# The first seven-product tile of each half layer: another order of its products, and one step of its sums of x moved

## The chip, the cores and the metric

The kernel runs on one core of a Trainium2 chip. The metric is the device time of one execution in microseconds; the time of a kernel is the median of its runs. Five engines take part: PE (TensorE, matmuls; PEld are its weight loads), DVE (VectorE), ACT (ScalarE), POOL (GpSimd) and SP (SyncE, which issues most of the DMAs). Each has its own list of instructions, and semaphores make one wait for another.

## The reference

One inference step of a two-layer decoder: 512 prompt tokens and 8 sample tokens, model width 1024, hidden width 2816, all in float32. Each layer is half a SwiGLU, a token mixer (causal pooling in layer 0, windowed attention in layer 1), and another half SwiGLU:

```python
def _rmsnorm(x, g):
    y = xf * lax.rsqrt(jnp.mean(xf * xf, axis=-1, keepdims=True) + EPS)
    return (y * g.astype(jnp.float32)).astype(x.dtype)

def _swiglu(x, wg, wu, wd):
    return (jax.nn.silu(x @ wg) * (x @ wu)) @ wd
...
        x = x + 0.5 * _swiglu(_rmsnorm(x, norm_g[l, 0]), ffn_w_gate[l, 0], ffn_w_up[l, 0], ffn_w_down[l, 0])
        h = _rmsnorm(x, norm_g[l, 1])
...
        x = x + 0.5 * _swiglu(_rmsnorm(x, norm_g[l, 2]), ffn_w_gate[l, 1], ffn_w_up[l, 1], ffn_w_down[l, 1])
```

So there are four SwiGLU blocks, called half layers 1 to 4 here (`fi` 0 to 3 in the code). They are most of the work and the place of the change.

## The kernel before

**Layout.** Activations are held transposed: the 1024 features in eight tiles of 128 partitions, and 520 tokens along the free dimension, cut into two halves of H = 260. Each value is split into a high part in fp32r (ScalarE, a copy) and a low part (VectorE, value minus high part), and each product is three matmuls: high x high, high x low, low x high (`terms`). Weights are split in the same way, in pieces of 128 x 512: L260 (ACT) makes `wh`, L261 (DVE) makes `wl`.

**Half layers.** The 2816 hidden features are 22 tiles of 128, in parts of 8, 8 and 6. For each part the gate and up tiles come first, one hidden tile j at a time, and then the down projection. The first NPL = (4, 3, 2, 3) hidden tiles of each half layer are plain (`plain_tile`: four pieces of weights, 24 matmuls each). From tile j = NPL on, `strassen_tile` computes gate and up together by a scheme of seven products of 2 x 2 blocks instead of eight. The blocks of the weights are A11, A12 (gate, lower and upper 512 features of x) and A21, A22 (up); the blocks of x are B11, B12 (lower features, token half 0 and 1) and B21, B22 (upper). The seven products, each 12 matmuls of 128x260 at L563, are A11 B11, S1 T1, S2 T2, A12 B21, S4 B22, S3 T3 and A22 T4. S1 to S4 are sums of weight blocks, T1 to T4 sums of x.

**Sums of the weights** (`Weights.combos`, `sums`). S1 and S3 are formed by accumulating DMAs on POOL's queue (L191, L192). S2 is S1 added onto A11 in place (L197, DVE), S4 is S2 added onto A12 in place (L201, DVE); so A11 must be split before S2 is formed, and A12 before S4. `sums` lists the pieces of a tile in the order in which the products take them: A11, S1, (A22 of the tile before), S2, A12, S4, S3; A22 follows in the next tile's list. Weights are split up to five pieces ahead (`prefetch`), in six buffers.

**Sums of x** (`sums` inside `yoco_step`, L780 to L801). A generator of eight steps, two for each k of 0 to 3. The first scales two tiles of x (L787, ACT, twice), makes t1 and t2 (L792, L793, DVE) and splits them into `th` and `tl` (L319, L320) as pair k; the second makes t3 and t4 (L797, L798) and splits them as pair k + 4. T1 and T2 are the halves of pairs 0 to 3, T3 and T4 those of pairs 4 to 7. L792 and L797 are kept in program order (`later`).

**Hooks.** A plain tile calls one hook after each piece of its weights. `start_hooks` gives the list for half layers 1, 2 and 4: `none` once or twice, `norm` (the norm's token sums, `rstd_tok`, and the first step), `none`, `norm_all` (the norm R over all tokens, and `known`, which releases the plain tiles that wait for R), and then seven steps. Half layer 3 starts its steps earlier, beside the K/V projection, and has a list of its own (L1288). `strassen_tile` is called after the remaining hooks are drained.

**Banks.** A double bank (`duo`) has two PSUM banks; four doubles rotate. A seven-product tile takes two: `a` is the first bank of one, `c` both of the other. A11 B11 opens `a`, and after the copy `sa` (L705) S2 T2 adds onto it. S1 T1 opens the second bank of `c`; after the copy `sb` (L707) S4 B22 adds onto it. A12 B21 opens the first bank of `c`. Then gate = silu of (`sa` + `c`) x R: L713, L714, L715. S3 T3 and A22 T4 go on adding in `a` for the up half (L717, L720, L722). The last product of a tile is delayed into the next one (`finish`).

**Order.** In these parts the order of the instructions on each engine is not that of the source: a planner lays it down when the kernel is built, by its own idea of durations, from the dependencies and the place in the source; it may mix the matmuls of two products or of two tiles. Only what is wrapped in `later` keeps its place.

## Time and profile before

| | us |
|---|---|
| median of 3 runs | 1655.13 |
| lowest and highest run | 1652.17, 1657.66 |
| the profiled execution | 1657.26 |
| its span, first to last instruction | 1655.5 |
| mean granted TensorE clock | 0.990 |

The costliest groups are these; a row gives line, engine, operation, names, shapes and count, then busy time, mean ns of one, and the engine's idle time just before them with what ended most of it.

```profile
L260 ACT ACTIVATE wh<-raw 128x512 fp32r<-128x512 f32 (+1 forms) x794 | 465.3, 619 | 262.7 <-PE ps L535 81.3
L261 DVE TENSOR_TENSOR wl<-raw,wh 128x512 fp32r<-128x512 f32 (+1 forms) x794 | 518.0, 675 | 71.1 <-ACT wh L260 69.1
L563 PE MATMUL ps<-th,wh 128*128 128x260 f32 x1216 | 343.7, 284 | 1.5 <-ACT wh L260 1.2
```

Times inside the execution are counted from the first instruction. The first seven-product tiles of the four half layers begin in this execution at 62.88, 438.10, about 802.5 and 1331.57.

### The profile page before, as it was taken

The page shows a single profiled execution, that of the slowest core. Times are in us where ns is not written, and L with a number is a line of the kernel's source. Part 1 is how long each engine was busy: PE and PEld are TensorE (multiplying, and loading weights), DVE is VectorE, ACT ScalarE, POOL GpSimd, SP SyncE. Part 2 cuts the span into 40 slices and gives each one's busy share as a digit, 9 for nine tenths or more (in the row PEclk, how much of TensorE's full clock was granted, in tenths as well). Part 3 has the DMA queues.
Part 4 walks back from the last instruction along what each step waited for, and adds up shares of the span by engine and source line. Part 5 has one row for each costly group of instructions (what it writes and reads, how often), then busy time and mean ns, then how long its engine had stood idle before and what let it go on. Part 6 is the DMA issues. An engine that isn't in the chain of part 4 may idle for free.

```text
span 1655.5 us, 34978 instructions
## 1 busy us (share of the span) xinstructions
PE 1624.3 (98%) x13386; PEld 1607.8 (97%) x13386; DVE 1421.8 (86%) x2817; ACT 980.1 (59%) x2032; POOL 228.9 (14%) x304
## 2 busy tenths in 40 slices
PE   9999999999999999999999999999989999999997
PEld 9999999999999999999999999999989999999997
DVE  6999999887899999888899989886786799999886
ACT  5665665566665565655655665655785565565555
POOL 1111111000111111100211111101110111111100
PEclk9999999999999999999999999999979999999999
DMA  8577878752587887744787877753222567787851
GB/s 225 119 174 180 183 175 176 192 158 87 127 181 176 179 185 176 163 134 103 186 186 178 182 175 173 170 181 91 59 50 75 126 142 176 179 184 173 178 139 52
DMA packets 377363, 254.62 MB, mean 154 GB/s; under 512 B 13134, under 2 KB 343878, under 8 KB 377156
## 3 DMA queue, kind: packets, MB, share of 16 engines
q1 hardware_dynamic: 339390, 187.30, 40.9%
q0 software_dynamic: 34048, 60.00, 22.7%
q10 hardware_dynamic: 3758, 5.09, 1.0%
q8 instruction: 105, 1.72, 0.4%
q14 instruction: 62, 0.51, 0.1%
HBM read 189.76 MB, written 6.11 MB: 118 GB/s over the span
## 4 chain that ended last, share of the span: by engine, by line
PE 90%; DVE 3%; ACT 3%; DMA 1%; issue 1%; POOL 0%; SPq 0%; DVEq 0%; ACTq 0%; POOLq 0%
PE ps L563 64%; PE ps L535 20%; ACT wh L260 1%; DVE wl L261 1%; PE ps L1464 1%; PE ps L1061 1%; DMA pr<-in_bands_dram 1%; PE ps L1086 1%; ACT sm L1408 1%; PE ps L1377 0%; PE ps L1433 0%; PE ps L494 0%; PE ps L1752 0%; PE ps L1759 0%; DMA raw<-in_ffn_w_gate_dram 0%
## 5 line engine op out<-in xcount | busy, mean ns | idle before, releaser
L260 ACT ACTIVATE wh<-raw 128x512 fp32r<-128x512 f32 (+1 forms) x794 | 465.3, 619 | 262.7 <-PE ps L535 81.3
L261 DVE TENSOR_TENSOR wl<-raw,wh 128x512 fp32r<-128x512 f32 (+1 forms) x794 | 518.0, 675 | 71.1 <-ACT wh L260 69.1
L563 PE MATMUL ps<-th,wh 128*128 128x260 f32 x1216 | 343.7, 284 | 1.5 <-ACT wh L260 1.2
L563 PE MATMUL ps<-th,wl 128*128 128x260 f32 x1216 | 342.4, 282 | 0.6 <-DVE wl L261 0.6
L563 PE MATMUL ps<-tl,wh 128*128 128x260 f32 x1216 | 342.3, 282 | 0.0
L563 PE MATMUL ps<-xh,wh 128*128 128x260 f32 x896 | 253.6, 284 | 3.3 <-ACT sb L707 1.8
L563 PE MATMUL ps<-xl,wh 128*128 128x260 f32 x896 | 251.6, 282 | 0.0
L563 PE MATMUL ps<-xh,wl 128*128 128x260 f32 x896 | 250.5, 282 | 0.5 <-DVE wl L261 0.4
L192 POOL DMA_DIRECT2D raw<-raw x108 | 93.1, 862 | 1046.8 <-DVE wl L261 283.5
L563 PEld LDWEIGHTS ps<-th,wh 128*128 128x128 f32 x1216 | 228.4, 188 | 3.7 <-ACT wh L260 2.5
L563 PEld LDWEIGHTS ps<-th,wl 128*128 128x128 f32 x1216 | 228.8, 188 | 0.8 <-DVE wl L261 0.8
L563 PEld LDWEIGHTS ps<-tl,wh 128*128 128x128 f32 x1216 | 229.0, 188 | 0.0
L563 PE MATMUL ps<-hh,wh 128*128 128x260 f32 x656 | 184.7, 285 | 2.4 <-ACT wh L260 1.8
L563 PE MATMUL ps<-hl,wh 128*128 128x260 f32 x656 | 183.8, 283 | 0.2 <-DVE hl L320 0.2
L563 PE MATMUL ps<-hh,wl 128*128 128x260 f32 x656 | 183.1, 282 | 0.0
L563 PEld LDWEIGHTS ps<-xh,wh 128*128 128x128 f32 x896 | 168.3, 188 | 5.3 <-ACT sb L707 2.2
L563 PEld LDWEIGHTS ps<-xh,wl 128*128 128x128 f32 x896 | 168.1, 188 | 0.9 <-DVE wl L261 0.9
L563 PEld LDWEIGHTS ps<-xl,wh 128*128 128x128 f32 x896 | 168.4, 188 | 0.0
L563 PEld LDWEIGHTS ps<-hh,wh 128*128 128x128 f32 x656 | 123.0, 188 | 4.3 <-ACT wh L260 2.8
L563 PEld LDWEIGHTS ps<-hl,wh 128*128 128x128 f32 x656 | 123.3, 188 | 0.4 <-DVE hl L320 0.4
L563 PEld LDWEIGHTS ps<-hh,wl 128*128 128x128 f32 x656 | 123.0, 188 | 0.0
L535 PE MATMUL ps<-hh,wh 128*128 128x260 f32 x572 | 116.3, 285 | 0.6 <-ACT vtok L1245 0.6
(331 smaller groups left out, 3595.2 us busy)
## 6 DMA issues: line engine op xcount, KB each, us to landing
raw<-in_ffn_w_gate_dram SPq DMA_DIRECT2D x87, 512.0 KB, 5.6
raw<-in_ffn_w_up_dram SPq DMA_DIRECT2D x87, 512.0 KB, 5.6
raw<-in_ffn_w_down_dram SPq DMA_DIRECT2D x128, 256.0 KB, 4.4
raw<-raw POOLq DMA_DIRECT2D x108, 256.0 KB, 3.5
S<-raw POOLq DMA_DIRECT2D x108, 256.0 KB, 4.6
S<-in_ffn_w_up_dram SPq DMA_DIRECT2D x76, 256.0 KB, 6.2
raw<-in_ffn_w_down_dram SPq DMA_DIRECT2D x16, 768.0 KB, 4.5
S<-in_ffn_w_down_dram SPq DMA_DIRECT2D x32, 256.0 KB, 4.5
```

Of the source, the lines that this page charges most:

```text
L192: G.dma_start(blk(raw, 2, 1), blk(raw, 1, 1), accum_op=ALU.add)
L260: pin(nc.scalar.activation(dh, src, AF.Copy))
L261: pin(nc.vector.tensor_tensor(dl, src, dh.bitcast(F32), op=ALU.subtract))
L535: ins = T.matmul(banks[:, hf, :H], a[:, kk, :], hcols(b, hf), start=(first and i == 0), stop=(last and i == 2),)
L563: T.matmul(bank[:, :H], a[:, kk, :], b, start=(not more and kk == 0 and i == 0), stop=(kk == 3 and i == 2), skip_group_check=more,)
L1061: T.matmul(o, a[:, s], b[:, kk, :], start=(n == 0), stop=(n == 5))
L1086: T.matmul(po[:, half * 256 : half * 256 + 256], z[:, tau, c], b, start=(i == 0), stop=(i == len(lst) - 1),)
L1408: S.activation(z, z, AF.Exp, scale=-1.0, bias=nm[:, i : i + 1], accum_out=self.den[:, i : i + 1])
L1464: T.matmul(po[:, bi * 256 : (bi + 1) * 256], a, p_[:, kc_], start=(n == 0), stop=(n == 3 * len(kts) - 1),)
```

## The change

It has four parts. (1) For the first seven-product tile of each half layer the weights' pieces are listed as A11, A12, S4, S1, S2, S3; S4's function forms S2 first, once, and S2's piece finds it formed. (2) `strassen_tile` takes the products of that tile in the same order: A11 B11, A12 B21, S4 B22 (all on x itself), then S1 T1, S2 T2, S3 T3, A22 T4. S4 B22 now opens its bank, and S1 T1 goes to the second bank of the double whose first bank is `a`. (3) Since S1 T1 is no longer added in the bank, one new VectorE instruction adds `sb` to the second half of `g`, between L713 and L714. (4) In the hooks of `start_hooks` the `none` between `norm` and `norm_all` becomes a step, and the list ends one step sooner; the number of steps is as before.

```diff
@@ combos
         def s2(raw):
-            V.tensor_tensor(blk(raw, 1, 1), blk(raw, 1, 1), tmp[1], op=ALU.add)
+            if "S2" not in tmp:
+                V.tensor_tensor(blk(raw, 1, 1), blk(raw, 1, 1), tmp[1], op=ALU.add)
+                tmp["S2"] = True
             return blk(raw, 1, 1)
 
         def s4(raw):
+            s2(raw)
             V.tensor_tensor(blk(raw, 1, 2), blk(raw, 1, 2), blk(raw, 1, 1), op=ALU.add)
             return blk(raw, 1, 2)
@@ Weights.sums
-    def sums(self, ch, again):
+    def sums(self, ch, again, first=False):
 
         v = self.combos(ch, again)
-        for name in ("A11", "S1"):
+        head, rest = (("A11", "A12"), ("S4", "S1", "S2", "S3")) if first else (("A11", "S1"), ("S2", "A12", "S4", "S3"))
+        for name in head:
             self.piece(ch, v[name])
         self.last()
-        for name in ("S2", "A12", "S4", "S3"):
+        for name in rest:
             self.piece(ch, v[name])
@@ plan_ffn
-                    W.sums(ch, ld(lambda t: t, u3[:, :4, c]))
+                    W.sums(ch, ld(lambda t: t, u3[:, :4, c]), j == NPL[2 * l + f])
@@ strassen_tile
-    def strassen_tile(tmp, xx, tt, hs):
+    def strassen_tile(tmp, xx, tt, hs, early=False):
...
-        a, c = duo()[:, 0, :], duo()
+        both, c = duo(), duo()
+        a, b = both[:, 0, :], both[:, 1, :] if early else c[:, 1, :]
         product(B(xx, lo, 0), a)
         S.copy(hcols(sa, 0), a[:, :H])
-        product(B(tt, lo, 0), c[:, 1, :])
-        S.copy(sb, c[:, 1, :H])
+        if early:
+            product(B(xx, up, 0), c[:, 0, :])
+            product(B(xx, up, 1), c[:, 1, :])
+        product(B(tt, lo, 0), b)
+        S.copy(sb, b[:, :H])
         finish()
         product(B(tt, lo, 1), a, True)
         S.copy(hcols(sa, 1), a[:, :H])
-        product(B(xx, up, 0), c[:, 0, :])
-        product(B(xx, up, 1), c[:, 1, :], True)
+        if not early:
+            product(B(xx, up, 0), c[:, 0, :])
+            product(B(xx, up, 1), c[:, 1, :], True)
         V.tensor_tensor(halves(g), halves(sa), c[:, :, :H], op=ALU.add)
+        if early:
+            V.tensor_tensor(hcols(g, 1), hcols(g, 1), sb, op=ALU.add)
         V.tensor_tensor(g, g, R, op=ALU.mult)
@@ ffn
-                    strassen_tile(tmp, mov, tt, hs)
+                    strassen_tile(tmp, mov, tt, hs, j == NPL[fi])
@@ start_hooks
-        return [none] * late + [norm, none, norm_all] + [step] * 7
+        return [none] * late + [norm, step, norm_all] + [step] * 6
```

## The prediction

> **What bounds the kernel now.** I read the page first, for its totals. Times are microseconds.
>
> ```profile
> span 1655.5 us, 34978 instructions
> ...
> PE 1624.3 (98%) x13386; PEld 1607.8 (97%) x13386; DVE 1421.8 (86%) x2817; ACT 980.1 (59%) x2032; POOL 228.9 (14%) x304
> ```
>
> PE is busy for 98% of the span, so a change that adds and removes no matmul can only win back PE's waits. Second, the waits of PE over the whole span: the longest entries at line 563, the seven-product matmuls.
>
> ```profile
> PE ps L563 <- ACT wh L260: 3.8, 6, 0.8
> PE ps L563 <- ACT sb L707: 1.8, 2, 1.4
> ...
> PE ps L563 <- DVE wl L261: 1.0, 2, 0.6
> ```
>
> Third, PE's timeline, to see where those waits lie. The `ps<-xh` row that starts at 62.88 (half layer 1) or at 438.10 (half layer 2) is the first matmul of the first seven-product tile; the others are what stalled behind it.
>
> ```profile
> 62.88 0.28 PE L563 MATMUL ps<-xh,wh 128*128 128x260 f32 x1
> ...
> 68.12 0.39 PE L563 MATMUL ps<-th,wh 128*128 128x260 f32 x1 [0.60 <-ACT wh L260]
> ...
> 73.50 0.39 PE L563 MATMUL ps<-xh,wh 128*128 128x260 f32 x1 [1.44 <-ACT sb L707]
> ...
> 438.10 0.28 PE L563 MATMUL ps<-xh,wh 128*128 128x260 f32 x1
> ...
> 441.45 0.39 PE L563 MATMUL ps<-xh,wl 128*128 128x260 f32 x1 [0.42 <-DVE wl L261]
> 443.53 0.39 PE L563 MATMUL ps<-th,wh 128*128 128x260 f32 x1 [0.60 <-ACT wh L260]
> 444.63 0.39 PE L563 MATMUL ps<-th,wl 128*128 128x260 f32 x1 [0.59 <-DVE wl L261]
> 448.27 0.39 PE L563 MATMUL ps<-xh,wh 128*128 128x260 f32 x1 [0.39 <-ACT sb L707]
> ```
>
> Nearly all of the listed wait sits in these two places. Because matmul ends are modelled, I size the loss by counting matmuls in stretches (busy us, number; then DVE, ACT, POOL).
>
> ```profile
> 62.00:74.00 12.00, 9.84 (x73) 8.84 (x72) 11.32 (x23) 8.28 (x18) 0.00 (x0) 1.00 0.01 1
> 74.00:107.00 33.00, 33.00 (x278) 33.00 (x277) 29.29 (x55) 19.84 (x41) 5.19 (x6) 1.00 0.78 183
> ...
> 437.00:450.00 13.00, 10.99 (x85) 10.15 (x84) 11.36 (x23) 8.86 (x18) 0.00 (x0) 1.00 0.01 4
> ...
> 804.00:866.00 62.00, 62.00 (x520) 62.00 (x519) 56.61 (x105) 38.92 (x78) 9.52 (x11) 1.00 0.75 170
> 1330.00:1344.00 14.00, 14.00 (x119) 14.00 (x118) 12.80 (x25) 9.21 (x19) 0.00 (x0) 1.00 0.36 95
> ```
>
> The undisturbed stretch gives 33.00 / 278 = 0.1187 for a matmul, 1.42 for a product of twelve. Then 62 to 74 lost 12.00 - 73 x 0.1187 = 3.33, and 437 to 450 lost 13.00 - 85 x 0.1187 = 2.91: 6.24 together. The first seven-product tiles of half layers 3 and 4 (from about 802.5, and in 1330 to 1344) lose nothing: 520 and 119 matmuls at that pace fill their stretches. So the ceiling of this change is about 6.2, and two of its four places can only cost.
>
> Fourth, the chain of waits through the first place, to see what is late.
>
> ```profile
> 67.44 0.64 ACT wh L260
> ...
> 72.03 1.15 ACT hh L319 x2
> 73.18 0.27 ACT sb L707
> 73.45 0.04 issue
> 73.50 2.54 PE ps L563 x19
> ```
>
> The place lies on the chain that ends the kernel, so time won there should carry to the end. The long wait is a bank that is not yet free: S4's product adds onto the bank that holds S1's, so the copy L707 must first take S1's product out, and ScalarE does two other splits (L319) before that copy. And the sums come late; VectorE's timeline has the pieces of `sums`:
>
> ```profile
> 38.16 0.42 DVE L792 TENSOR_TENSOR t<-xa 128x260 f32<-128x260 f32 x1
> ...
> 53.54 0.42 DVE L797 TENSOR_TENSOR t<-xb,xa 128x260 f32<-128x260 f32 x1
> ...
> 57.29 0.42 DVE L797 TENSOR_TENSOR t<-xb,xa 128x260 f32<-128x260 f32 x1
> 57.63 0.42 DVE L798 SCALAR_TENSOR_TENSOR t<-t,xb 128x260 f32<-128x260 f32 x1
> ...
> 69.09 1.30 DVE L320 TENSOR_TENSOR tl<-t,th 128x520 fp32r<-128x520 f32 x2
> ...
> 445.17 1.49 DVE L320 TENSOR_TENSOR tl<-t,th 128x520 fp32r<-128x520 f32 x2
> ```
>
> The first step runs at 38.16, its second half (L797) only at 53.54; the last two low parts `tl` (pairs 3 and 7) are done at 70.39, about 7.5 after the tile that needs them began.
>
> ```profile
> 34.00:44.00 10.00, 10.00 (x87) 10.00 (x86) 5.92 (x19) 4.71 (x9) 2.07 (x3) 1.00 0.93 191
> ...
> 50.00:62.00 12.00, 12.00 (x102) 12.00 (x101) 11.90 (x24) 8.75 (x16) 3.96 (x6) 1.00 0.73 165
> ...
> 107.00:115.00 8.00, 7.67 (x59) 7.05 (x58) 8.00 (x18) 5.60 (x14) 1.70 (x2) 1.00 0.77 169
> ...
> 407.00:419.00 12.00, 12.00 (x103) 12.00 (x102) 8.93 (x25) 6.32 (x12) 0.00 (x0) 1.00 0.42 110
> 419.00:437.00 18.00, 18.00 (x152) 18.00 (x152) 16.74 (x42) 12.37 (x23) 4.58 (x6) 1.00 0.67 147
> ...
> 449.00:518.00 69.00, 69.00 (x577) 68.86 (x575) 64.66 (x121) 40.51 (x85) 11.59 (x14) 1.00 0.79 180
> ```
>
> VectorE is idle for 10.00 - 5.92 = 4.08 in 34 to 44, but for 0.10 in 50 to 62: it runs out just where the sums are made, after having had time.
>
> **The change part by part.** *Order of the products.* Before, T (sums of x) is needed from the second product on; after, from the fourth, two products or 2.84 later. In place 1 the fourth product would start at 62.88 + 3 x 1.42 = 67.14 and need pair 3 nine matmuls later, at 68.21. The pair of `tl` from 69.09 takes 0.65 each, so pair 3 is done at 69.74 today, 1.53 too late; pair 7, needed by the sixth product at 71.05, is done at 70.39, in time. The wait for the bank goes altogether: S4's product now starts its own bank, S1's goes to the second bank of the other double, and the copy L707 has no matmul behind it. What can be late next on that bank pair is S2's product, which still adds onto A11's after the copy L705; it starts at 68.56, 4.3 after A11's product ends at 64.30.
>
> *The step in the empty hook.* Half layers 1, 2 and 4 issue the second half of the first pair one hook earlier, ahead of the norm's end and of the delayed tiles that `known` releases; half layer 3 has its own hooks and keeps them. It issues two adds 0.34 apart (57.29 to 57.63) and a low part of 0.65: 0.34 + 0.34 + 0.65 = 1.33 of VectorE, and one split on ScalarE, half of the 1.15 that two took at 72.03; no DMA. VectorE's idle time in 34 to 44 (4.08) and 407 to 419 (12.00 - 8.93 = 3.07) hides it, and every later step moves up a hook. If VectorE just gains 1.33, pair 3 in place 1 is done at 68.41: residual wait 0.2. In place 2 the fourth product starts at 438.10 + 4.26 = 442.36 and needs pair 3 at 443.43; it is done at about 445.9 today, so at 444.6: residual 1.1, or 0 if the earlier hooks also use the 18.00 - 16.74 = 1.26 that VectorE idles in 419 to 437. I take 0.6, the middle.
>
> *The weights' sums.* S2's add (L197) stays third, S4's add (L201) goes from fifth piece to third, in each of the four places; the DMAs that form S1 and S3 keep their order on POOL's queue and are needed no sooner, since S1 was second before.
>
> ```profile
> L201 DVE TENSOR_TENSOR raw<-raw x108: 677/683/693, 59.5 to 1595.5; 128x512 f32<-128x512 f32 x108
> ```
>
> It stands 0.68 on VectorE, moved and not added. Behind it wait the split of S4 and the sums' steps; at 50 to 62 they are many microseconds ahead of their use. Taken 0, bounds 0 and 0.68 a place.
>
> *The added add* (128x260, both operands in SBUF) is not in the trace; the nearest row is L797 with the same shape. It costs 0.34 if it overlaps its neighbour, 0.42 alone. The silu and the hidden split wait for it, and these are due at the end of the part, near 107 in place 1. Taken 0 on the path, 0.42 a place if the cover is gone. [...]
>
> *What PE runs into sooner.* It reaches the end of the gate tiles 3.1 earlier in place 1 (3.33 - 0.2). VectorE must then do the same work sooner: 3.1, less the 1.33 done early, plus 0.42, is 2.2 out of 33.00 - 29.29 = 3.71 idle in 74 to 107. At 107 to 115 VectorE has no idle time, and PE loses 8.00 - 59 x 0.1187 = 1.00 already. Some of the idle time cannot be used: I take 0.5 lost (bounds 0 and 2.2). In place 2 it is 2.3 - 1.33 + 0.42 = 1.4 out of 69.00 - 64.66 = 4.34: 0.3 lost (bounds 0 and 1.4).
>
> *Sum.* 3.33 - 0.2 - 0.5 = 2.6, and 2.91 - 0.6 - 0.3 = 2.0: **4.6 us**. The profiled execution took 1657.26 (1655.5 of span and 1.76 around it), 2.13 over the median of the runs; it would be 1652.7, and the median 1655.13 - 4.6 = **1650.5**. By the bounds the gain ends at 6.24 - 0.2 - 1.1 - 2.2 - 0.9 = 1.8 below (0.9 being what place 2 can lose later when it won only 1.8 first), at -0.4 if the other two places pay 0.42 + 0.68 each as well, and at 6.2 above.
>
> **Rivals.** *All of it goes.* The earlier steps use all idle time, pair 3 is in time in both places, and even the 1.00 at 107 shrinks: gain 5.6 to 7.2, so 1648 to 1649.5. For it: VectorE idles in both places before the crowded stretch. Against: 50 to 62 has 0.10 left.
>
> *The wait only moves.* VectorE is the true limit of the gate tiles, and PE waits at 104 to 112 for what it no longer waits for at 68 to 73: gain 1 to 3, 1652 to 1654. For it: 8.00 of 8.00 busy at 107. Against: 3.71 idle before.
>
> *Slower: VectorE's fixed order.* All that moves forward or is new stands ahead of weight splits that PE waits for: 0.68 + 0.42 in four places and 1.33 in three, 4.4 + 4.0 = 8.4 if nothing of it is hidden and nothing won, 1663.5. It decides from the point where VectorE has no idle time left in the stretch where it lands; with the forecast's gains beside it the time is 1655.13 + 8.4 - 4.6 = 1658.9, so more than 0.3% slower needs most of the gains gone too. [...] Against the rival: the idle 4.08 and 3.07.
>
> *It doesn't do what it says.* The order on PE is laid down by the planner; the `xh,wl` of 441.45 shows it mixing products of the next tile in. Then nothing moves: 1654 to 1656.
>
> **Chances.** Forecast (gain 3.4 to 5.6) 0.42, all of it 0.28, only moves 0.15, slower 0.12, nothing 0.03. A difference of 0.3%, or 5.0, is about what a measurement of this kernel can tell. Faster by more: 0.28 and 0.17 of the forecast's 0.42, 0.45. Slower by more: 0.08 of the 0.12. Within: the other 0.25 of the forecast, 0.15, 0.04 and 0.03, 0.47. The forecast's own range is 1649.5 to 1651.7; 1647.5 to 1656 adds the other gains and the edge of no gain, and leaves out the slower case and the best of the second.
>
> **What would show it.** The wait of PE on `sb` L707 at about 73 and 448 gone; 36 matmuls on `xh`, `xl` in one run before the first `th`; L797 near 40 and not at 53.5; the count of PE's matmuls in the twelve microseconds around the tile's start (62 to 74) near 12 / 0.1187 = 101 instead of 73; the same places in half layers 3 and 4 unchanged. It is wrong if PE's waits near 68 to 69 stay, or if as much appears at 104 to 112.

## The result, and the profile after

| | before | after |
|---|---|---|
| median, us | 1655.01 (6 runs, 1651.68 to 1660.18) | 1644.28 (6 runs, 1640.43 to 1645.45) |
| ratio to before | | 0.9932, 95% interval 0.9911 to 0.9952 |
| profiled execution, us | 1657.26 | 1640.43 |
| its span, us | 1655.5 | 1638.3 |
| its mean granted clock | 0.990 | 0.996 |

The change wins 10.7 us, 7.9 to 14.7 by the interval: faster, as the forecast's own case said, but by more than twice its 4.6, and the median lies below 1647.5, the low end of the range. The profiled executions differ by more than the medians do, 17.2 in span: that of the changed kernel is the lowest of its six runs, and the rest of why is part of what follows. Lines below 197 stand 3 to 11 further down in the changed kernel: L563 is L567, L260 is L264, L261 is L265, L707 is L715, L320 is L324, L797 is L808.

The waits of PE over the whole span of the changed kernel (releaser, then total us, times, longest):

```profile
PE ps L567 <- ACT wh L264: 1.8, 3, 0.8
...
PE ps L567 <- DVE sb L728: 0.5, 1, 0.5
```

The 1.8 on `sb` L707 and the 1.0 on `wl` are gone, and the 3.8 on `wh` is 1.8. PE's timeline of the changed kernel at the first place, its first tile from 63.10 on:

```profile
63.10 0.28 PE L567 MATMUL ps<-xh,wh 128*128 128x260 f32 x1
...
67.53 0.28 PE L567 MATMUL ps<-xl,wh 128*128 128x260 f32 x1
67.64 0.28 PE L567 MATMUL ps<-th,wh 128*128 128x260 f32 x1
...
68.96 0.28 PE L567 MATMUL ps<-xh,wl 128*128 128x260 f32 x1
...
```

No row in it has a wait. The matmuls on `xh` and `xl` run without a break from 63.10 to 67.53 (38 rows: the three products and two more), then those on the sums of x begin, and from 68.96 to 70.28 the planner slips further matmuls on x in. That is where the sums are late, as VectorE's timeline shows:

```profile
38.73 0.42 DVE L808 TENSOR_TENSOR t<-xb,xa 128x260 f32<-128x260 f32 x1
...
68.27 0.70 DVE L324 TENSOR_TENSOR tl<-t,th 128x520 fp32r<-128x520 f32 x1
...
69.48 0.70 DVE L324 TENSOR_TENSOR tl<-t,th 128x520 fp32r<-128x520 f32 x1
```

The early step runs at 38.73, in the gap that VectorE had there. The last low parts still end at 68.97 and 70.18 (69.74 and 70.39 before), but PE has other work until then. The counts of matmuls by stretch (busy us and number of PE, PEld, DVE, ACT, POOL; clock; DMA):

```profile
62.00:74.00 12.00, 12.00 (x103) 12.00 (x102) 10.72 (x22) 8.28 (x18) 0.89 (x1) 1.00 0.49 120
74.00:107.00 33.00, 33.00 (x278) 32.98 (x277) 32.05 (x61) 20.02 (x41) 5.77 (x7) 1.00 0.75 179
107.00:115.00 8.00, 7.57 (x61) 7.18 (x60) 7.95 (x17) 6.49 (x15) 1.16 (x2) 1.00 0.44 80
...
434.00:447.00 13.00, 12.55 (x103) 12.15 (x102) 10.77 (x22) 9.59 (x20) 0.68 (x1) 1.00 0.48 116
446.00:515.00 69.00, 68.64 (x571) 68.31 (x570) 65.85 (x125) 41.78 (x85) 12.10 (x14) 1.00 0.74 171
```

At 0.1187 for a matmul, 62 to 74 loses nothing (3.33 before), 107 to 115 loses 0.76 (1.00 before), and the second place, which comes 3.4 sooner here, loses 13.00 - 103 x 0.1187 = 0.77 (2.91 before).

**Stage by stage.** From the trace of each profiled kernel I took the time from the first seven-product matmul of a half layer to the first matmul of the norm after it (for half layer 4, to the end of PE's last matmul), and for the attention stage between half layers 3 and 4 from its first matmul on scores (L1377, L1388) to the norm. This is the only view in which kernels with different shifts can be laid beside each other:

| us | half layer 1 | 2 | 3 | attention | 4 |
|---|---|---|---|---|---|
| before | 309.72 | 324.49 | 327.71 | 152.00 | 314.77 |
| before, two more profiles | 310.67, 309.80 | 325.14, 323.00 | 327.13, 326.64 | 152.07, 152.05 | 314.35, 313.87 |
| after | 306.04 | 320.76 | 325.43 | 144.41 | 314.69 |
| after, two more profiles | 306.52, 307.16 | 321.85, 321.92 | 325.45, 325.37 | 144.54, 144.58 | 315.21, 315.67 |

By the means of three, half layer 1 gains 3.5, half layer 2 gains 2.7, half layer 3 gains 1.7, half layer 4 loses 0.9: 7.0 together. The four add up to between 1273.3 and 1277.3 in the profiles of before and to between 1266.9 and 1270.1 in those of the changed kernel, so the 7.0 is uncertain by 2 to 3 (an estimate from that scatter), and the 0.9 of half layer 4 is no more than its profiles scatter. The other stretches agree within 0.3, but for the one ahead of the first tile (62.7 to 63.9) and the one from the end of half layer 1 through the token mixer to the next norm (39.2 to 41.8), which vary from profile to profile whatever the kernel. And the attention stage, which the change doesn't touch, is 7.5 shorter in the profiles. In the rest of this text these are the two questions: where in the half layers the 7.0 come from, and what the 7.5 are.

### The profile page after: what moved, and what is told of

It is laid out like the page before. It is cut to its first block, busy times and chain, and to the rows that moved or that the text cites. A ratio compares the mean times of both kernels' runs of the same rounds, so it can differ in the third digit from the quotient of the medians.

```text
span 1638.3 us, 35023 instructions
## 1 busy us (share of the span) xinstructions
PE 1612.4 (98%) x13386; PEld 1598.0 (98%) x13386; DVE 1422.0 (87%) x2821; ACT 979.3 (60%) x2032; POOL 229.1 (14%) x304
## 4 chain that ended last, share of the span: by engine, by line
PE 90%; DVE 3%; ACT 3%; DMA 1%; issue 1%; POOL 0%; DVEq 0%; ACTq 0%; POOLq 0%
PE ps L567 64%; PE ps L539 22%; DVE wl L265 1%; PE ps L1072 1%; DMA S<-raw 1%; ACT sm L1419 1%; PE ps L1097 1%; DMA xt<-in_x_prompt_dram 1%; ACT wh L264 1%; ACT xh L323 0%; PE ps L1475 0%; PE ps L498 0%; PE ps L1763 0%; ACT oT L1494 0%; PE ps L1388 0%
## 5 line engine op out<-in xcount | busy, mean ns | idle before, releaser
L264 ACT ACTIVATE wh<-raw 128x512 fp32r<-128x512 f32 (+1 forms) x794 | 464.0, 618 | 264.8 <-DVE raw L198 77.8
L265 DVE TENSOR_TENSOR wl<-raw,wh 128x512 fp32r<-128x512 f32 (+1 forms) x794 | 520.9, 679 | 71.0 <-ACT wh L264 69.3
L567 PE MATMUL ps<-th,wh 128*128 128x260 f32 x1216 | 343.7, 283 | 1.0 <-DVE sb L728 0.5
L567 PE MATMUL ps<-tl,wh 128*128 128x260 f32 x1216 | 342.2, 282 | 0.0
L567 PE MATMUL ps<-th,wl 128*128 128x260 f32 x1216 | 342.0, 282 | 0.0
L567 PE MATMUL ps<-xh,wh 128*128 128x260 f32 x896 | 252.2, 283 | 0.8 <-ACT wh L264 0.7
L567 PE MATMUL ps<-xl,wh 128*128 128x260 f32 x896 | 251.4, 282 | 0.0
L567 PE MATMUL ps<-xh,wl 128*128 128x260 f32 x896 | 250.5, 282 | 0.0
L567 PEld LDWEIGHTS ps<-th,wh 128*128 128x128 f32 x1216 | 228.7, 188 | 2.4 <-DVE sb L728 0.7
L567 PEld LDWEIGHTS ps<-tl,wh 128*128 128x128 f32 x1216 | 228.9, 188 | 0.0
L567 PEld LDWEIGHTS ps<-th,wl 128*128 128x128 f32 x1216 | 228.5, 188 | 0.0
L567 PE MATMUL ps<-hh,wh 128*128 128x260 f32 x656 | 184.8, 284 | 2.0 <-ACT wh L264 1.1
L567 PE MATMUL ps<-hl,wh 128*128 128x260 f32 x656 | 184.0, 283 | 0.2 <-DVE hl L324 0.2
L567 PE MATMUL ps<-hh,wl 128*128 128x260 f32 x656 | 183.2, 282 | 0.0
L567 PEld LDWEIGHTS ps<-xh,wh 128*128 128x128 f32 x896 | 168.1, 188 | 1.8 <-ACT wh L264 1.8
L567 PEld LDWEIGHTS ps<-xl,wh 128*128 128x128 f32 x896 | 168.3, 188 | 0.0
L567 PEld LDWEIGHTS ps<-xh,wl 128*128 128x128 f32 x896 | 168.1, 188 | 0.0
L567 PEld LDWEIGHTS ps<-hh,wh 128*128 128x128 f32 x656 | 123.1, 188 | 3.5 <-ACT wh L264 1.8
L567 PEld LDWEIGHTS ps<-hl,wh 128*128 128x128 f32 x656 | 123.2, 188 | 0.4 <-DVE hl L324 0.4
L567 PEld LDWEIGHTS ps<-hh,wl 128*128 128x128 f32 x656 | 122.9, 188 | 0.0
```

What stands on the lines that cost most here:

```text
L264: pin(nc.scalar.activation(dh, src, AF.Copy))
L265: pin(nc.vector.tensor_tensor(dl, src, dh.bitcast(F32), op=ALU.subtract))
L567: T.matmul(bank[:, :H], a[:, kk, :], b, start=(not more and kk == 0 and i == 0), stop=(kk == 3 and i == 2), skip_group_check=more,)
```

## The experiments

**One part of the change at a time.** e1_order is the change without its last hunk, e2_hook is that hunk alone:

```diff
-        return [none] * late + [norm, none, norm_all] + [step] * 7
+        return [none] * late + [norm, step, norm_all] + [step] * 6
```

> Order of the products and of the weights' pieces changed in all four half layers, the hooks as before. Theory (the bank's wait and the later need of T do the work, the hook little): half layers 1 and 2 from their first seven-product matmul to their end each 2 to 3.5 us shorter than before (309.72 and 324.49 in the profile of before), half layer 3 about 2.3 shorter as in the changed kernel. Rival (the hook is what counts, because VectorE is late with pairs 3 and 7): half layers 1 and 2 at most 1.5 us shorter each, with a wait of PE for pair 3 of about 1.5 left in the first tile. Total: theory 6 to 9 us faster, rival 3 to 5, apart from the attention stage.

> Only the hooks: the second half of the first pair one hook earlier, the products in the order of before. Theory: the wait for the copy sb (1.4 in half layer 1, 0.4 in half layer 2) stays, and of the rest of the 6.2 us lost there 1 to 2.5 go; half layer 3 changes by under 0.5, since its hooks are not touched. Rival (the hook counts): 4 us or more in half layers 1 and 2 together. Total: theory 1 to 3 us faster, rival 4 to 6, apart from the attention stage.

e3_third has the order of products changed in half layer 3 alone, with the hooks of before, and e4_again is the kernel before, unchanged, for the scatter between profiles of one text.

```diff
-                    strassen_tile(tmp, mov, tt, hs, j == NPL[fi])
+                    strassen_tile(tmp, mov, tt, hs, fi == 2 and j == NPL[fi])
```

> Order changed in half layer 3 alone, hooks as before. Its first tile had no wait, so a gain there comes from another place. Theory (the planner lays the later tiles of the same half layer out otherwise, and waits at the ends of its parts go): half layer 3 from its first seven-product matmul to the attention is 2.3 us shorter (before 327.71, changed kernel 325.43), half layers 1 and 2 as before within 0.3. Rival (the 2.3 us come from what half layers 1 and 2 hand on to it): half layer 3 as before within 0.5.

> The kernel before, profiled once more, for the attention stage, which the change doesn't touch and which took 152.00 us in the profile of before and 144.41 in that of the changed kernel, with the granted clock at half for 24 us in the one and 3.4 in the other. Theory (where the half-clock windows fall changes from execution to execution): the stage takes another time here, anywhere from 144 to 153, with a different number of 3.4 us windows. Rival (the change itself shifts the stage against the windows, the same in each execution): 152.0 within 0.5 again, clock 0.990. Ratio to before 1.000.

| | median, us | ratio, 95% interval | half layer 1 | 2 | 3 |
|---|---|---|---|---|---|
| e1_order | 1647.74 | 0.9959, 0.9941 to 0.9978 | 309.93 | 320.44 | 325.85 |
| e2_hook | 1648.96 | 0.9966, 0.9948 to 0.9984 | 307.44 | 324.32 | 326.39 |
| e3_third | 1653.12 | 0.9996, 0.9974 to 1.0018 | 308.89 | 323.45 | 325.58 |
| e4_again | 1654.72 | 1.0000, 0.9982 to 1.0017 | 310.67 | 325.14 | 327.13 |

The two half layers answer to different parts. Half layer 1 gains nothing from the order and 2.6 from the hook (310.06, the mean of the three profiles of before, less 307.44); half layer 2 gains 3.8 from the order and nothing from the hook. So neither the theory nor the rival of these two runs holds in both places. PE's waits of e1_order inside half layer 1 tell why; beside them those of the kernel before and of the changed one in the same half layer:

```profile
PE ps L567 <- ACT xh L323: 1.2, 1, 1.2
PE ps L567 <- ACT wh L264: 1.1, 2, 0.7
PE ps L567 <- ACT sa L747: 1.0, 1, 1.0
...
PE ps L567 <- ACT sb L715: 0.8, 1, 0.8
```

```profile
PE ps L563 <- ACT sb L707: 1.4, 1, 1.4
PE ps L563 <- ACT wh L260: 1.3, 2, 0.7
```

```profile
PE ps L567 <- DVE sb L728: 0.5, 1, 0.5
PE ps L567 <- ACT sa L747: 0.4, 1, 0.4
```

With the order alone the wait on `sb` shrinks and turns up again as `xh`, `sa` and `wh`, at 107.02, 111.48 and 114.97, near the 104 to 112 where the second rival had put them (the larger wait on `wh`, 0.7 near 237, stands in the kernel before too). The counts of e1_order, and under them those of e2_hook, in the same three stretches:

```profile
62.00:74.00 12.00, 11.51 (x93) 11.02 (x91) 11.19 (x24) 8.16 (x16) 0.87 (x1) 1.00 0.43 103
74.00:107.00 33.00, 31.16 (x258) 30.95 (x258) 29.78 (x57) 20.48 (x42) 5.19 (x6) 1.00 0.72 160
107.00:115.00 8.00, 6.65 (x52) 6.24 (x52) 7.02 (x16) 4.47 (x10) 1.72 (x2) 1.00 0.72 144
```

```profile
62.00:74.00 12.00, 11.45 (x94) 11.09 (x93) 11.87 (x24) 8.68 (x17) 0.00 (x0) 1.00 0.26 63
74.00:107.00 33.00, 33.00 (x277) 33.00 (x277) 29.96 (x57) 19.20 (x40) 5.17 (x6) 1.00 0.78 180
107.00:115.00 8.00, 8.00 (x69) 8.00 (x68) 7.30 (x16) 5.76 (x14) 1.71 (x2) 1.00 0.66 141
```

Over 62 to 115 the kernel before runs 410 matmuls (73, 278, 59), e1_order 403, e2_hook 440, the changed kernel 442. So in half layer 1, by these counts, VectorE's and ScalarE's time is the limit: another order of the products only moves PE's wait, and work done in the gap at 38 is what takes it away. In half layer 2 it is the other way round. e2_hook keeps the waits there, and the order alone removes most of them; the three profiles of the changed kernel, 320.76 to 321.92, are no shorter there than e1_order's 320.44. PE's timeline of e2_hook, then of e1_order, in the second place:

```profile
441.17 0.39 PE L563 MATMUL ps<-xh,wl 128*128 128x260 f32 x1 [0.39 <-DVE wl L261]
443.24 0.39 PE L563 MATMUL ps<-th,wh 128*128 128x260 f32 x1 [0.60 <-ACT wh L260]
447.72 0.39 PE L563 MATMUL ps<-xh,wh 128*128 128x260 f32 x1 [0.39 <-ACT sb L707]
```

```profile
444.66 0.71 PE L567 MATMUL ps<-th,wh 128*128 128x260 f32 x2 [0.35 <-ACT th L323]
```

**The bank alone, and more of the hook.** e5_bank keeps the old order and the old hooks, but gives S1 T1 the bank beside A11's, with the added VectorE instruction; e6_two is the changed kernel with two steps in the moved hook and one fewer behind; e7_after_again and e8_third_again are the changed kernel and e3_third once more.

```diff
-        product(B(tt, lo, 0), c[:, 1, :])
-        S.copy(sb, c[:, 1, :H])
+        product(B(tt, lo, 0), b)
+        S.copy(sb, b[:, :H])
...
+        if early:
+            V.tensor_tensor(hcols(g, 1), hcols(g, 1), sb, op=ALU.add)
```

> The products in the order of before and the hooks of before; only S1's product goes to the second bank of the other double, so that S4's need not wait for the copy sb, and the added add follows. Theory (two causes in half layers 1 and 2: the bank, worth 1.6 and 0.55, and the late T, worth the rest): half layer 2 from its first seven-product matmul to its end is 0.4 to 0.9 shorter than before (mean of three executions of the same code 324.4), not the 3.8 of the new order; half layer 1 (mean 309.8) 0 to 1.6 shorter, the rest coming back at the end of its first part. Rival (the bank is all): half layer 2 shorter by 3 or more. Half layer 3 (mean of three 327.1; 325.6 with the new order): if its 1.5 come from the planner laying out later tiles anew, whatever small edit there is, it changes by something between -2 and +2 here too; if they come from the order of the products, it stays within 0.5 of 327.1.

```diff
-        return [none] * late + [norm, step, norm_all] + [step] * 6
+        def two():
+            step()
+            step()
+
+        return [none] * late + [norm, two, norm_all] + [step] * 5
```

> The changed kernel with two steps in the moved hook instead of one, the list one shorter again. Theory (what is left in half layer 2's first tile, 0.9 us in waits for pair 3's th and the copy sa, is the sums being late): that wait goes, half layer 2 is 0.5 to 1 shorter than in the changed kernel (320.76), half layer 1 within 0.7 of 306.04; total 0.995 to 1.0 of the changed kernel. Rival (VectorE and ScalarE are needed for the norm in that slot): the norm's end, about 20 us before the tile, comes later, and the plain tiles before the first seven-product tile take over 0.3 longer (25.35 in half layer 2).

> The changed kernel once more. Half layers 1, 2, 3 within 1.0 of 306.04, 320.76 and 325.43: the gain there stays. Theory (the attention stage takes what the clock windows of that execution give): 144 to 153 in it, and a total that differs from the profile of the changed kernel by that much. Rival (the changed kernel always has the good attention stage): 144.4 within 0.3.

> The kernel with the new order in half layer 3 alone, once more. Its first profile had no half-clock window in the attention stage (144.43) and was the lowest of ten runs by 3.4 us. Theory (the windows change by execution): a different time in that stage, with the clock at half in some of it, up to 153. Rival (the program decides): 144.4 within 0.3. Half layer 3 again 325.6 within 0.7.

| | median, us | ratio, 95% interval | half layer 1 | 2 | 3 |
|---|---|---|---|---|---|
| e5_bank | 1649.64 | 0.9956, 0.9938 to 0.9973 | 310.76 | 322.97 | 325.77 |
| e6_two | 1650.84 | 0.9986, 0.9969 to 1.0003 | 308.16 | 321.59 | 326.30 |
| e7_after_again | 1642.74 | 0.9926, 0.9904 to 0.9947 | 306.52 | 321.85 | 325.45 |
| e8_third_again | 1651.78, one run | | 310.22 | 323.68 | 326.15 |

The bank alone wins nothing in half layer 1 and 1.2 in half layer 2, a little above the 0.4 to 0.9 of its theory; most of its waits have other names, and 0.8 on the copy `sb` is left, now before a matmul on `th` (PE's waits inside half layer 1 of e5_bank; L708 is that copy there):

```profile
PE ps L563 <- ACT wh L260: 1.1, 2, 0.7
PE ps L563 <- ACT sa L739: 1.0, 1, 1.0
PE ps L563 <- ACT sb L708: 0.8, 1, 0.8
...
```

That the bank was the cause of the long wait, as the prediction had it, is true only of the wait's name: where the bank is free, PE waits elsewhere for as long. Two early steps are worse than one: half layer 1 gains 1.9 instead of 3.5, and PE waits again near 109, in e6_two's timeline:

```profile
109.25 0.39 PE L567 MATMUL ps<-hh,wh 128*128 128x260 f32 x1 [0.96 <-ACT sa L747]
```

What in VectorE's or ScalarE's order makes that copy late was not traced. It isn't a late norm: the plain tiles ahead of the first seven-product tile of half layer 2 take 25.35 in e6_two as in every kernel, so the rival of that run fails with its theory. e7 gives the result of the change again. e5's median is 5.4 below that of before, while its four half layers add up to 0.5 less than before in its profile; where the rest comes from is not shown.

**An edit that does nothing.** Half layer 3 has no wait at its first tile and keeps its hooks, and yet it gains 1.7 in the changed kernel, and 1.6 and 1.0 in the two profiles of e3 and e8, where only its own order is changed. e9_add puts one VectorE add into the kernel before, with a result that nobody reads, in the first seven-product tile of half layer 3; e10_copy does it with a ScalarE copy. e11 and e12 are further single runs of before and after.

```diff
+        if extra:
+            V.tensor_tensor(hcols(t, 1), hcols(g, 1), sb, op=ALU.add)
```

> The kernel before, with one added add in the first seven-product tile of half layer 3 alone; its result (into the second half of t, which the silu overwrites) is used by nothing. Products, weights, banks and hooks as before. Theory (half layer 3 gains 1.4 because the planner lays the later tiles out anew after any small edit): half layer 3 is not 327.1 here but nearer 325.7, or as far off on the other side; PE's waits at the ends of its parts change. Rival (the gain needs the product order or the bank): 327.1 within 0.5, and an added add costs 0 to 0.4.

> The same with a copy on ScalarE in place of the add, again used by nothing. Theory: half layer 3 takes another time than 327.1 by 0.7 or more, in either direction, though the edit can only cost. Rival: 327.1 within 0.5.

> The kernel before, a third look. Theory (the attention stage's time is set by where its start falls in the 3.413 us grid of the clock's windows, counted from the first full-clock window): from the looks so far, a start at 0.25 to 0.8 of a window gives 144.4 to 144.6, at 0.95 to 0.0 about 146, at 0.1 about 152, at 0.17 about 149. This look lies on that curve within 0.7. Rival (the program decides): 152.0 again, wherever the start falls. Half layers 1 to 3: 309.9, 324.2 and 327.1, each within 1.

> The changed kernel, a third look. Half layers 1 to 3: 306.3, 321.3 and 325.4, each within 0.8. The attention stage on the same curve as for the kernel before within 0.7; rival (the program decides): 144.5 within 0.3 wherever its start falls.

One run each: e9_add 1650.16, e10_copy 1652.12, e11_before_look 1655.53, e12_after_look 1644.76, a run of the kernel before beside them 1656.90. Half layer 3 took 324.59 in e9_add, 2.6 less than before with one instruction more, and 326.26 in e10_copy. In the trace of e10_copy every other instruction of PE, VectorE and ScalarE in the half layers stands in the order of before: the planner laid nothing out anew, and this is a fourth profile of the layout of before, which so scatters from 326.26 to 327.71. In that of e9_add PE's order is another one in half layer 3, and that of before in the other three. PE's waits inside half layer 3, of the kernel before, of e9_add and of the changed kernel:

```profile
PE ps L563 <- ACT wh L260: 0.8, 1, 0.8
PE ps L563 <- ACT sa L744: 0.6, 1, 0.6
PE ps L563 <- DVE g L722: 0.4, 1, 0.4
```

```profile
PE ps L563 <- DVE xl L320: 0.2, 1, 0.2
```

```profile
PE ps L567 <- ACT wh L264: 0.7, 1, 0.7
```

None of these is at the first tile; they stand between 984 and 1012, far behind it, and two of the three go with the layout unchanged: e10_copy has 0.7 on `wh` alone. Its 326.26 is the 0.8 off 327.1 that its theory asked for, without the new layout that was to bring it. In e9_add an edit of one instruction made the planner lay out the tiles behind it in another way, and the wait on `wh`, which all profiles of before have, went too. So half layer 3's gain doesn't need the new order of the products: an unused add brings it too, in the one profile there is. That add stands where the changed kernel has its own new add, so whether the layout does it or an add in this place is not told apart.

**The attention stage.** PE's instructions there are the same in every kernel. Two things are not: the order which the planner gives VectorE and ScalarE, call it A in the kernel before and B in the changed one, and the place where the stage begins on a grid of 3.413 us, on which the granted clock changes between 1.00 and 0.50: in the trace of before it changes at 1192.76, 1196.17, 1213.24, 1220.07, 1226.89 and 1240.55, steps of 1, 5, 2, 2 and 4 times 3.413. The place is counted from the start of the first full-clock window. That the stage changes from execution to execution, the theory of e4_again, e7_after_again and e8_third_again, holds for the last alone (146.15 after 144.43): three profiles of the kernel before agree within 0.1 there, and three of the changed one within 0.2. The last four kernels are to separate order and place. They have some unused fill matmuls ahead of the stage, about 0.22 us each (in the trace of before a fill is two records at L529 that start 0.11 apart at the full clock); their number decides which order comes out, and outside that stage the orders of VectorE and ScalarE stay as they were.

```diff
             if h == 0:
                 qb[t] = duo()
+            if (t, h) == (0, 0):
+                fill(qb[t][:, 0, :], 5)
             q_half(qb[t], 4 * h)
```

> The kernel before with 5 unused fill matmuls (about 0.23 us each, 1.2 in all) ahead of the attention stage; VectorE and ScalarE keep the order of the kernel before in the whole program. The stage should begin about 0.35 of a window later on the grid, near 0.45 instead of 0.06 to 0.11. If the place on the grid sets the time of the stage, it takes 144.5 to 147.5 instead of 152.0 and the kernel comes out 3 to 6 us below the kernel before; if the order sets it, it takes 152.0 again and the kernel comes out 1.2 above.

> The kernel before with 10 such fills (2.3 us): VectorE and ScalarE have, in the attention stage alone, the order of the changed kernel; everything else is as before. The stage should begin near 0.8 on the grid. By the order, and by the place too, it takes 144.5 to 146 and the kernel comes out 3.5 to 5 below the kernel before, although the half layers are those of before. If it takes 149 or more, neither holds.

> The changed kernel with 18 such fills (4.2 us): VectorE and ScalarE have, in the attention stage alone, the order of the kernel before; everything else is as in the changed kernel. The stage should begin near 0.68 on the grid. By the order it takes 152 and the kernel comes out about 0.5 above the kernel before (10.7 won, 4.2 and 7.5 lost); by the place it takes 144.5 to 146 and the kernel comes out 5 to 7 below.

> The changed kernel with 9 such fills (2.1 us): the order of the changed kernel in the attention stage but for two instructions; the stage should begin near 0.05 on the grid, where that of the kernel before begins. By the place it takes 149 to 152 and the kernel comes out 1 to 3 below the kernel before; by the order it takes 144.5 to 146 and the kernel comes out 7 to 9 below.

| | order | begins at (share of 3.413) | attention, us | median, us | ratio, 95% interval |
|---|---|---|---|---|---|
| before, e4, e11 | A | 0.11, 0.10, 0.06 | 152.00, 152.07, 152.05 | | |
| e13_a_five | A | 0.49 | 147.45 | 1655.11 | 1.0001, 0.9985 to 1.0018 |
| e10_copy | A | 0.45 | 147.45 | | |
| e15_a_eighteen | A | 0.15 | 145.89 | 1649.47 | 0.9980, 0.9958 to 1.0003 |
| e9_add | A but for a few instructions | 0.08 | 146.31 | | |
| after, e7, e12 | B | 0.40, 0.47, 0.46 | 144.41, 144.54, 144.58 | | |
| e3, e8 | B | 0.29, 0.96 | 144.43, 146.15 | | |
| e14_b_ten | B | 0.63 | 144.69 | 1654.66 | 0.9994, 0.9973 to 1.0015 |
| e5_bank | B | 0.75 | 144.58 | | |
| e16_b_nine | B, two instructions off | 0.72 | 147.67 | 1647.42 | 0.9962, 0.9946 to 0.9979 |
| e1_order, e2_hook | a third | 0.44, 0.97 | 144.56, 145.95 | | |
| e6_two | a fourth | 0.17 | 149.21 | | |

The fills moved the stage by other amounts than I had worked out, since they take 0.2 to 4.0 in the stretch ahead, so e15 and e16 didn't land where they were meant to. They still answer. Neither theory holds alone: order A takes 152.0, 147.45 or 145.89, and at 0.45 to 0.49 A takes 147.45 where B takes 144.5. Nor do the two together give a curve: at 0.08, between the 0.06 and 0.10 where A takes 152.05 and 152.07, e9_add takes 146.31 with all but a few instructions in the order A. The totals expected of e13_a_five and e14_b_ten, 3 to 6 and 3.5 to 5 below the kernel before, didn't come: their medians are 1.3 and 0.8 above the 1653.84 beside them, although the stage took 147.45 and 144.69 in their profiles. Within the order A the time goes with the clock. Here is the whole stage in the kernel before, in e13_a_five, in e14_b_ten and in the changed kernel:

```profile
1148.76:1300.76 152.00, 145.14 (x1188) 140.17 (x1188) 113.96 (x336) 104.91 (x284) 20.94 (x39) 0.92 0.31 73
```

```profile
1150.88:1298.33 147.45, 140.52 (x1189) 135.54 (x1189) 113.86 (x336) 104.70 (x284) 21.01 (x39) 0.95 0.32 76
```

```profile
1153.72:1298.41 144.69, 139.27 (x1189) 134.28 (x1188) 113.61 (x336) 104.56 (x284) 21.43 (x39) 0.96 0.32 77
```

```profile
1139.38:1283.79 144.41, 136.88 (x1189) 131.30 (x1188) 113.62 (x336) 104.44 (x284) 21.17 (x39) 0.99 0.32 77
```

The number of matmuls and the work of VectorE and ScalarE are equal; the granted clock (third number from the end) is 0.92, 0.95, 0.96 and 0.99; e15_a_eighteen, order A too, has 0.96. The last two take nearly the same time at different clocks, and e3_third, order B with a clock of 1.00, takes 144.43 as well. That would fit slow windows that fall where PE waits anyway, which was not shown. So the clock alone doesn't give the time either: at 0.96 the order B takes 146.15 in e8_third_again, and e6_two takes 149.21 at 0.97.

The medians say how much of the 7.5 is in the timed runs. The fills cost what half layer 3 grew by (its mean in the profiles of before is 327.16, of after 325.42): 327.32, 330.74, 329.40 and 327.44 in e13 to e16, that is 0.2, 3.6, 4.0 and 2.0. Without that the medians would be 1654.9, 1651.1, 1645.5 and 1645.4. So the order of the changed kernel is worth 3.8 in the half layers of before (e14 against e13) and 0.1 in those of the changed kernel (e16 against e15), each with an uncertainty of some 3. Two earlier kernels are split in the same way: e5_bank and e3_third both have order B, and half layers that by their profiles add up to 0.5 and 2.1 less than before; one won 5.4 and the other 0.9, which leaves 4.9 and -1.2 for the rest. A gain of 0 to 4 is about what these bear out, and not 7.5. And e15, the changed kernel with the order A, is without its fills still 8.3 below the 1653.84 of the runs of before beside it: most of the win doesn't need the order B.

The mean clocks of the timed runs say the same. The three profiles of before have 0.990; of the 88 timed runs of before whose clock is on record, 9 have 0.990 or less, so most of them ran less long at the slow clock than the profiles. The 7 with 0.990 have a median of 1658.9 and the 34 with 0.994 or more one of 1651.8, so one and the same program moves by 7.1 with its clock, nearly the 7.5; in which stage, the timed runs can't show. The mean clock over those 88 was 0.9931, and 0.9941 over 11 runs of the changed kernel. A straight line through the 88 falls by 1.1 us for each 0.001 of clock, so by this estimate the clock gave about 1 of the 10.7. At an equal clock, 0.993 to 0.996, 49 runs of before have a mean of 1653.3 and the 11 of the changed kernel one of 1643.9: 9.3 apart. That is above the 7.0 of the half layers, but within what their profiles leave uncertain.

## Why the prediction was right and wrong

**The step that failed** is the ceiling: "the ceiling of this change is about 6.2, and two of its four places can only cost". It rests on the reading that nearly all of the listed wait sits at the first tiles of half layers 1 and 2, and that is not so: of the 6.6 listed, 4.0 lie there, and 2.6 of the 3.8 on `wh` lie further on, at 236.71, 621.78, 993.25 and 1389.68; two of these in PE's timeline of the kernel before:

```profile
621.78 0.39 PE L563 MATMUL ps<-hh,wh 128*128 128x260 f32 x1 [0.76 <-ACT wh L260]
...
993.25 0.39 PE L563 MATMUL ps<-xh,wh 128*128 128x260 f32 x1 [0.76 <-ACT wh L260]
```

Every gain outside the first tiles was put at nothing, and the runs show some there: 1.7 in half layer 3, about 1 by the clock (an estimate), and the later waits of half layer 2. In place of 2.6 + 2.0 = 4.6 the half layers won 3.5 + 2.7 + 1.7 - 0.9 = 7.0. That alone would have given 1648.1, inside the range; the other 3.7 took the median out of it. About 1 of the 3.7 goes with the clock, and where the rest comes from stays open.

**What held.** The forecast's own case was a gain, and there is one; by its classes, though, a change within 5.0 had 0.47 and faster by more 0.45. The wait on `sb` L707 is gone in both places, the products on x run in one piece, the second half of the first pair stands at 38.73 in the gap that was to hide it, and 62 to 74 has 103 matmuls where "near 101" was said. Nothing of note appears at 68 to 69, 0.4 at 107.94, and the first tiles of half layers 3 and 4 keep their 520 and 119 matmuls. The moved adds of the weights, the added add and the moved step cost nothing that shows in half layers 1 and 2.

**Place 1** was put at 3.33 - 0.2 - 0.5 = 2.6; half layer 1 gains 3.5. Neither deduction came. The residual of 0.2 was argued from a strict order of the products; the late pair is indeed later (68.97 against 68.41), but the planner covers it with matmuls on x from 68.96 to 70.2. The 0.5 "lost later" had the wrong sign: 74 to 107 has the same 278 matmuls, and 107 to 115 loses 0.76 instead of 1.00, as the rival "all of it goes" had said; 3.33 and 0.24 make up the 3.5. VectorE there is busy for 32.05 of 33.00 instead of 29.29: it had the time for it. e1_order shows that the fear was right without the hook, so the term was mis-sized for the sum of both parts, not for the order by itself.

**Place 2** was put at 2.91 - 0.6 - 0.3 = 2.0; half layer 2 gains 2.7. The first part is as worked out: 2.14 of the 2.91 went, and 0.77 is left for the 0.6 allowed. In 446 to 515 it lost 69.00 - 571 x 0.1187 = 1.2 against 0.5 before, more than the 0.3. What made up for that lies further on, where the prediction hadn't looked: PE's waits of half layer 2 before and after are

```profile
PE ps L563 <- ACT wh L260: 1.4, 2, 0.8
PE ps L563 <- DVE wl L261: 1.0, 2, 0.6
PE ps L563 <- ACT sa L744: 0.7, 1, 0.7
...
```

```profile
PE ps L567 <- ACT wh L264: 0.4, 1, 0.4
PE ps L567 <- ACT sa L710: 0.3, 1, 0.3
...
```

The 0.8 on `wh` at 621.78, which all three profiles of before have, and the 0.7 on `sa` L744 at 640.58, which two of them have, are gone; the other two profiles of the changed kernel have a new 0.6 on `g` L733 near 493. That half layers 1 and 2 together win 6.2, the number of the ceiling, is therefore in part luck. For half layer 2 the credit was given to the wrong part: the hook, taken for a gain of 1.33 on VectorE in both places, wins nothing there by itself.

**Places 3 and 4**, "can only cost", is wrong for half layer 3, which gains 1.7, and not decided for half layer 4, whose loss of 0.9 is within its scatter. The ceiling of 6.24 was a sum over the waits at the first tiles, on the tacit assumption that the layout elsewhere stays; in the kernels whose products or hooks changed it doesn't, and e9_add shows a gain of that size from an edit without purpose. The range of "all of it goes", 5.6 to 7.2, holds the 7.0 of the half layers, but not for its reason: it put nothing in half layer 3.

**What the prediction didn't have** is the attention stage and the granted clock. It read a clock of 1.00 in the stretches that it looked at and left the 0.990 of the page aside, and it took its own sum against an execution in which that stage was at its slowest. By the pairs above the medians owe the stage 0 to 4, and by the clocks about 1. With the 7.0 of the half layers that is 7 to 11, and 10.7 was measured (10.3 by the medians of the 88 and the 11 runs). What share the order has in it, what the place on the grid, and how much of it is the uncertainty of the 7.0, stays open.

**The rivals.** That the wait only moves is what half layer 1 does under the order alone (e1_order). The order in which VectorE's instructions stand may be what e6_two runs into, where 1.6 of the 3.5 are lost; which instruction stands in the way was not traced. No variant that ran beat the changed kernel.

## What to carry to other kernels

A change with two parts can need both in one place and only one of them in another, so try them apart in each place before crediting either. Where a planner orders the instructions, the waits at the place of an edit are no ceiling for it: lay the whole kernel side by side in stages, and run an edit that does nothing (one unused add) to see how far a new layout alone moves the time, after making sure in its trace that the order did change: one such edit moved a stage by 2.6, the other left the order as it was. And compare medians over many runs, with the mean granted clock beside them, before a difference between two profiles is put down to the code.

## What the hardware showed that was not expected

In the traces of before and after the granted clock falls to 0.50 for one, two or four windows of 3.413 us at a time, and in the attention stage of the kernel before four in a row are slow. PE's clock by stretch there, the third number from the end:

```profile
1223.40:1226.80 3.40, 2.36 (x25) 2.06 (x21) 2.53 (x11) 3.33 (x11) 0.00 (x0) 1.00 0.68 133
1226.90:1230.30 3.40, 3.40 (x17) 3.40 (x17) 3.34 (x12) 1.88 (x7) 0.44 (x1) 0.50 0.01 2
...
1237.10:1240.50 3.40, 3.40 (x18) 3.40 (x18) 2.96 (x17) 2.47 (x10) 1.60 (x2) 0.50 0.95 214
1240.60:1244.00 3.40, 3.40 (x31) 3.40 (x30) 2.16 (x4) 2.15 (x6) 0.00 (x0) 1.00 0.47 87
```

After a window in which PE was busy for only 2.36 of 3.40, the clock is 0.50 for 13.65 us and 1.00 again at 1240.55; in three profiles of this program it happened each time, and in e15_a_eighteen, with the same instructions and orders in the stage and a beginning 0.04 of a window further on than in the profile of before, it didn't happen (the mean clock of the stage is 0.96 there and 0.92 in the profile of before). The window just ahead doesn't decide it: in the profile of before PE is busy for 2.05 of 3.40 from 1203.00 to 1206.40 and the clock stays at 1.00 in the next, and in e13_a_five a slow window follows one with 3.40 of 3.40 (1231.10 to 1234.50). The slow stretches last 3.41 (from 373.56 and 1192.76 before, from 370.00 and 1206.27 after), 6.83 (from 1213.24 before) and 13.65 (from 1226.89 before), one, two or four times 3.413, on one grid in each trace, but for the last (from 1650.14 before and 1632.93 after), which the end of the kernel cuts off. PE shows as busy through each of the four slow windows of before, while one such window was enough in the changed kernel (3.30 of 3.30 from 1206.30 to 1209.60, 1.00 from 1209.68 on) and in e13_a_five (3.30 of 3.30 from 1234.60 to 1237.90). The ends of matmuls are modelled, so how busy PE was at the slow clock is not shown; why it took four in the one place was not settled, and what sets the clock was not shown.
